# Grouping the small matrix products of a state-space scan and a chunk gate between the large ones

## The chip, the cores and the metric

The kernel runs on one core of a Trainium2 chip. The metric is the device time of one execution in microseconds, as the median of several runs; the profile is of one execution by itself, taken by the hardware profiler.

## The reference

One decoder layer is computed for 256 new prompt positions and for 8 sequences with 8 new tokens each, 320 tokens in all. Everything is float32. The two parts of the layer:

```python
h = rms_norm(x, norm_mix_pre)
a_u, a_v, z, xbc, dt_raw = split(h @ w_in)
gate_out = gelu(a_u) * (tril(W_s) @ layer_norm(gelu(a_v)) + b)      # 16 heads, chunks of 128
ssm_out  = group_norm(ssd(silu(conv(xbc)), dt) * silu(z))           # 32 heads of 64, 4 groups, state 128
x = x + rms_norm([gate_out | ssm_out] @ w_out)
x = x + rms_norm(conv_ffn(rms_norm(x)))                             # 2048 -> 2 x 5632 -> 2048
```

The state-space part (`ssd`) is the recurrence h_t = exp(dt_t a) h_{t-1} + dt_t x_t B_t^T, y_t = h_t C_t, in chunks of 128 positions. With the decays within a chunk as a matrix, y of a chunk is (C B^T * decay) (dt x) plus C times the state that the chunk begins with. The prompt has two chunks and begins with a zero state, so its second chunk alone needs a state; each of the 8 sequences brings a state of its own (8 x 32 x 64 x 128 numbers) and has one short chunk. A group of 8 heads shares its B and C.

## The kernel before, in words

Channels lie on the partitions and the 320 tokens in the free dimension. Weights pass through the kernel once, in slabs of 128 x 1024 numbers (512 KB): `slab` loads one from SP's queue into `wraw`, ScalarE rounds it to `whi` (L119), VectorE makes the rest `wlo` (L121); each of the three has three buffers. `accumulate` (L130 to L132) turns a block of 128 x 128 weights into three products with 320 columns, `whi` x hi, `whi` x lo, `wlo` x hi, which keep float32's precision on the faster format. A slab is 24 such large products. `project` runs one projection of 512 columns, `chunk_out` one part of `w_out` or `ffn_w_down`; `pd` and `ps` are their PSUM banks (`mm`, four). All other products, in plain float32 and in two passes each, go to four banks of their own (`ms`, `misc`).

What isn't a large product is written as generators: `gate_mix(g)` for four heads of the gate, `ssd(g)` for a group of eight heads of the scan, and others. They wait in a list `bg`, and `tick` runs the first of them up to its next `yield`. `project` and `chunk_out` call `tick` once or more (`rate`) behind each slab. So the number of `yield`s settles behind which slab a small product stands in TensorE's order. A scheduler then places each engine's instructions by their priority in the program and its own estimates; each engine works through its own in that order, and waits in it.

The parts that the change and the prediction's steps touch:
- `gate_mix`: for each of four heads, products of the chunk weights with v (L663, L664, bank `sg`), then VectorE's and ScalarE's work on `s` and its split in hi and lo. It yields behind every second head. The last group's call is finished without ticks in between.
- `ssd`, begin: the tokens are transposed (`xt_ps`), C B^T goes to `cb`, and the eight state tiles `st` of the group (two for each `i`, 256 KB each) are asked for on SP's queue. There are eight buffers.
- `ssd`, `with_c(i, st)` (L812): C of the sequences times the states of one pair, four products of 32 array columns each, accumulated in the bank `yo_ps` over i = 0..3. Behind the last, VectorE puts the result into `xdt` (L822).
- `decays(hl)`: the decay matrix of one head. `load_sums` brings the sums of a pair of heads (`cs`, three buffers, 320 KB, SP's queue); VectorE takes differences (L844), ScalarE the exponential (L846), VectorE multiplies by `cb` (L848). For each pair ScalarE and GpSimd make `cpx` (L837, L838, two buffers).
- `products(j)` (L859, bank `y_ps`): y of a pair of heads, each head on 64 of the array's columns, in four terms; VectorE then writes y (L869).
- `decayed(1, 1)` on GpSimd (L788), s1 times decay on GpSimd (L880), and `final` (L885, bank `fin_ps`): the last state's product and VectorE's sum with s1 (L887), and the store of s1 from ScalarE's queue (L888).
- `heads_out`: the projection for z, in whose evacuation `finish(tasks[g])` runs what is left of the group's scan.

Of the kernel before, what the change touches and what calls it, by code (L numbers as in the profile page):

```python
# [34 lines left out]
def hybrid_step(  # L35
# [21 lines left out]
    def misc(name):  # L57
        return ms.tile([P, 512], F32, tag="ms", name=name)
# [283 lines left out]
    def split(hi, lo, x, scale=None):  # L342

        if scale is None:
            act.copy(hi, x)
            dve.tensor_tensor(out=lo, in0=x, in1=hi.bitcast(F32), op=ALU.subtract)
        else:
            made = act.activation(hi, x, AF.Copy, scale=scale).ins
            dve.scalar_tensor_tensor(out=lo, in0=x, scalar=scale, in1=hi.bitcast(F32), op0=ALU.mult, op1=ALU.subtract)
            return made  # L350

    def out_parts(pool_, name):
        return (pool_.tile([P, 4, NT], F32R, tag=f"{name}hi", name=f"{name}hi"),
                pool_.tile([P, 4, NT], F32R, tag=f"{name}lo", name=f"{name}lo"))
# [7 lines left out]
    def by_head(ap):  # L362
        return ap.rearrange("p (h d) -> p h d", d=64)
# [7 lines left out]
    with ExitStack() as mctx:  # L371
# [145 lines left out]
        with tc.tile_pool(name="gp", bufs=1) as gp:  # L517
# [124 lines left out]
            def gate_mix(g, uf, res):  # L642
                wT = gp.tile([P, 4, P], F32, tag="wT", name="wT", bufs=1)
                w8 = gp.tile([NS, 4, TS], F32, tag="w8", name="w8", bufs=1)
                bs = gp.tile([P, 4, P], F32, tag="bs", name="bs", bufs=1)
                with tc.issue_after(after_v[-1]):
                    pool.dma_start(wT, gate_wT[:, 4 * g:4 * g + 4, :])
                    pool.dma_start(w8, gate_w8[:, 4 * g:4 * g + 4, :])
                    pool.dma_start(bs, gate_b_s[0:1, 4 * g:4 * g + 4, :].broadcast_to([P, 4, P]))
                yield  # L650
                with tc.issue_after(rsqrt_ins[1]):
                    dve.tensor_tensor(out=wT, in0=wT, in1=upper.unsqueeze(1).to_broadcast([P, 4, P]), op=ALU.mult)
                    for j in range(4):
                        dve.tensor_tensor(out=wS[:NS, j], in0=w8[:, j].unsqueeze(1).to_broadcast([NS, NB, TS]),
                                          in1=upper_s[:NS].rearrange("p (b t) -> p b t", b=NB), op=ALU.mult)
                yield
                hi, lo = out_parts(hp, "o")
                res += hi, lo
                for j in range(4):
                    fs = slice(512 * g + P * j, 512 * g + P * j + P)  # L660
                    ps = misc("sg")
                    for c in range(2):
                        pe.matmul(ps[:, P * c:P * c + P], vt[:, c, fs], wT[:, j, :], start=True, stop=True)  # L663
                    pe.matmul(ps[:, NP:NT], vt[:, 2, fs], wS[:, j].rearrange("p b t -> p (b t)"), start=True, stop=True)  # L664
                    s = tp.tile([P, NT], F32, tag="ev", name="s", bufs=2)
                    dve.tensor_tensor(out=s[:, :NP].rearrange("p (c t) -> p c t", c=2),
                                      in0=ps[:, :NP].rearrange("p (c t) -> p c t", c=2),
                                      in1=bs[:, j, :].unsqueeze(1).to_broadcast([P, 2, P]), op=ALU.add)
                    dve.tensor_tensor(out=s[:, NP:].rearrange("p (b t) -> p b t", b=NB),
                                      in0=ps[:, NP:NT].rearrange("p (b t) -> p b t", b=NB),  # L670
                                      in1=bs[:, j, :TS].unsqueeze(1).to_broadcast([P, NB, TS]), op=ALU.add)
                    dve.tensor_tensor(out=s, in0=s, in1=uf[:, j, :], op=ALU.mult)
                    split(hi[:, j, :], lo[:, j, :], s)
                    if j % 2:
                        yield

            spare_pads = op.tile([P, 4, NT], F32, tag="xs", name="xs_pads", bufs=2).rearrange("p k n -> p (k n)")
            spare_pads = [spare_pads[:, LP * i:LP * i + LP] for i in range(3)]
# [23 lines left out]
        with tc.tile_pool(name="sd", bufs=1) as sd:  # L702
# [24 lines left out]
            def ssd(g):  # L727
# [58 lines left out]
                def decayed(i, c):  # L786
                    xde = sd.tile([P, 512], F32, tag="xde", name="xde", bufs=1)
                    pool.tensor_tensor(out=by_head(xde), in0=by_head(xdt[:, c, :]),  # L788
                                      in1=dec[:, i, h0:h0 + 8].unsqueeze(2).to_broadcast([P, 8, 64]), op=ALU.mult)
                    return xde  # L790
# [16 lines left out]
                def with_c(i, st):  # L807

                    for r in range(2):
                        for h in range(2):  # L810
                            row = 64 * r + 32 * h
                            pe.matmul(ps_yo[row:row + 32, :256], cms[:, 4 * h + i, :], st[h][:, 256 * r:256 * r + 256],  # L812
                                      start=i == 0, stop=i == 3, tile_position=(0, row))

                for i in range(4):
                    yield
                    with_c(i, sts[i])
                    yield

                for r in range(2):  # L820
                    at = slice(64 * r, 64 * r + 64)
# [9 lines left out]
                def decays(hl):  # L831
                    j, i = hl // 2, hl % 2
                    at = places(hl)
                    if i == 0:
                        cs = load_sums(j)
                        cpx = sd.tile([P, 2, P], F32, tag="cpx", name="cpx", bufs=2)
                        act.activation(cpx, cs[:, :, at[1][0]:at[1][0] + P], AF.Exp)  # L837
                        pool.tensor_tensor(out=cpx, in0=cpx, in1=cT[:, g, P:2 * P].unsqueeze(1).to_broadcast([P, 2, P]),  # L838
                                           op=ALU.mult)
                    else:  # L840
                        cs, cpx = made[hl - 1][1:]
                    m = cs[:, i]
                    for c, (o, n) in enumerate(at):
                        dve.tensor_scalar(out=m[:, o:o + n], in0=m[:, o:o + n], scalar1=nda[:, c, h0 + hl:h0 + hl + 1],  # L844
                                          scalar2=0.0, op0=ALU.add, op1=ALU.min)
                    act.activation(m, m, AF.Exp)  # L846
                    o = NS * (hl // 4)
                    dve.tensor_tensor(out=m, in0=m, in1=cb[:, o:o + NT], op=ALU.mult)  # L848
                    made[hl] = m, cs, cpx

                def products(j):

                    ps = misc("y_ps")
                    pair = [(i, *made[2 * j + i]) for i in range(2)]

                    def both(cols, w, x, **flags):
                        for i, m, _, cpx in pair:
                            hl = 2 * j + i
                            pe.matmul(ps[64 * i:64 * i + 64, cols], w(hl), x(hl, m, cpx), tile_position=(0, 64 * i), **flags)  # L859

                    def hs(hl):
                        return slice(64 * hl, 64 * hl + 64)
                    c0, c1, sm = (slice(o, o + n) for o, n in places(2 * j))
                    both(slice(0, P), lambda hl: xdt[:, 0, hs(hl)], lambda hl, m, cpx: m[:, c0], start=True, stop=True)
                    both(slice(P, NP), lambda hl: xdt[:, 1, hs(hl)], lambda hl, m, cpx: m[:, c1], start=True, stop=False)
                    both(slice(P, NP), lambda hl: s1[:, hs(hl)], lambda hl, m, cpx: cpx[:, hl % 2, :], start=False, stop=True)
                    both(slice(NP, NT), lambda hl: xdt[:, 2, hs(hl)], lambda hl, m, cpx: m[:, sm], start=True, stop=True)
                    y = xs[:, j, :]
                    dve.scalar_tensor_tensor(out=y, in0=y, scalar=d_col[:, 4 * g + j:4 * g + j + 1], in1=ps[:, :NT],  # L869
                                             op0=ALU.mult, op1=ALU.add)  # L870
                for j in range(5):
                    for i in range(2):
                        if j < 4:
                            decays(2 * j + i)
                        if j and i == 0:
                            products(j - 1)
                        yield

                x1d = decayed(1, 1)
                pool.tensor_tensor(out=by_head(s1), in0=by_head(s1),  # L880
                                   in1=dec[:, 2, h0:h0 + 8].unsqueeze(2).to_broadcast([P, 8, 64]), op=ALU.mult)

# [7 lines left out]
                if g == 3:  # L890
                    rest.append(final())
                else:
                    yield
                    yield
                    for _ in final():
                        pass

            tasks = [ssd(g) for g in range(4)]
            res = [[] for _ in range(4)]
# [402 lines left out]
```

## Time and profile before

| | |
|---|---|
| median of 3 runs | 1789.76 us (1789.74 to 1791.35) |
| the profiled execution | 1790.97 us, span 1789.3 us |
| TensorE busy | 1775.5 us (99%) |
| VectorE busy | 1191.2 us (67%) |
| ScalarE busy | 794.3 us (44%) |
| GpSimd busy | 276.6 us (15%) |
| granted clock of TensorE | 0.998 |
| bytes moved | 303.83 MB, 170 GB/s on the mean |

The span goes from the first to the last instruction; the time of the execution is somewhat longer. In the profile PE is TensorE's matrix products, PEld its weight loads, DVE VectorE, ACT ScalarE, POOL GpSimd, SP the engine whose queue issues most loads. A float32 product has two records, one for each pass. The scan (`ssd`) runs from about 430 to 730 us, between projections and parts of `w_out`; the gate from about 265 to 435 us.

### The profile page before, as it was taken

Reading aid. Unit: us, or ns where it says so; the run is one execution under the profiler, and the core shown is the slowest. Engines: PE = TensorE matmul, PEld = TensorE weight load, DVE = VectorE, ACT = ScalarE, POOL = GpSimd, SP = SyncE. Lnnn points to the kernel's source line nnn. Section 1 sums busy time; section 2 is a strip of 40 time slices with the busy share of each in tenths; the row PEclk is TensorE's granted clock in tenths of the full one; section 3 lists DMA queues with packets and bytes.
Section 4 is the critical chain, followed back from the end, with each engine's and each line's share of the span. In section 5 each row is a group of like instructions: output and inputs, shape, how many; then the busy total and the mean of one; then the engine's idle time right before and its main releaser. Section 6 shows DMA issues by size and latency. Waiting matters only on the chain.

```text
span 1789.3 us, 31254 instructions
## 1 busy us (share of the span) xinstructions
PE 1775.5 (99%) x12241; PEld 1744.7 (98%) x12241; DVE 1191.2 (67%) x2058; ACT 794.3 (44%) x1101; POOL 276.6 (15%) x591
## 2 busy tenths in 40 slices
PE   9999999999999999999999999999999999999998
PEld 9999999999999898999999999999999999999997
DVE  7448664557867778577866675767666575656565
ACT  6343455333535364445645434443434343433334
POOL 2003200000210111002322212121101020101004
PEclk9999999999999999999999999999999999999999
DMA  7455544445664644454565656566554444444442
GB/s 246 144 165 165 189 148 153 153 153 179 226 198 147 201 154 151 142 170 153 161 196 191 206 181 202 182 197 206 183 185 154 153 147 153 156 149 149 154 156 95
DMA packets 228082, 303.83 MB, mean 170 GB/s; under 512 B 17408, under 2 KB 149856, under 8 KB 227744
## 3 DMA queue, kind: packets, MB, share of 16 engines
q1 hardware_dynamic: 216288, 281.89, 49.4%
q10 hardware_dynamic: 10160, 15.47, 2.4%
q0 software_dynamic: 1488, 4.49, 0.8%
q8 instruction: 96, 1.57, 0.4%
q14 instruction: 50, 0.41, 0.1%
HBM read 284.23 MB, written 17.58 MB: 169 GB/s over the span
## 4 chain that ended last, share of the span: by engine, by line
PE 92%; DVE 4%; DMA 1%; issue 1%; ACT 1%; POOL 0%; SPq 0%; DVEq 0%; ACTq 0%; POOLq 0%
PE ps L130 19%; PE ps L132 19%; PE ps L131 19%; PE pd L130 10%; PE pd L132 10%; PE pd L131 10%; DVE wlo L121 1%; PE y_ps L859 1%; PE yo_ps L812 1%; PE tsum L264 0%; PE sg L663 0%; PE up_ps L1152 0%; DMA wraw<-in_w_in 0%; DVE acc_mix L998 0%; PE xt_ps L360 0%
## 5 line engine op out<-in xcount | busy, mean ns | idle before, releaser
L121 DVE TENSOR_TENSOR wlo<-wraw,whi 128x1024 fp32r<-128x1024 f32 x472 | 588.7, 1248 | 385.3 <-ACT whi L119 382.6
L119 ACT CAST whi<-wraw 128x1024 fp32r<-128x1024 f32 x472 | 494.2, 1047 | 726.1 <-PE ps L131 430.7
L130 PE MATMUL ps<-h_hi,whi 128*128 128x320 f32 x2528 | 784.5, 311 | 2.8 <-DVE dtf L430 2.1
L131 PE MATMUL ps<-h_lo,whi 128*128 128x320 f32 x2528 | 780.4, 309 | 0.0
L132 PE MATMUL ps<-h_hi,wlo 128*128 128x320 f32 x2528 | 779.4, 309 | 0.5 <-DVE wlo L121 0.2
L130 PEld LDWEIGHTS ps<-h_hi,whi 128*128 128x128 f32 x2528 | 474.6, 188 | 8.4 <-issue 3.8
L131 PEld LDWEIGHTS ps<-h_lo,whi 128*128 128x128 f32 x2528 | 474.8, 188 | 1.5 <-issue 0.5
L132 PEld LDWEIGHTS ps<-h_hi,wlo 128*128 128x128 f32 x2528 | 474.1, 188 | 2.0 <-DVE wlo L121 1.8
L130 PE MATMUL pd<-fhi,whi 128*128 128x320 f32 x704 | 217.3, 309 | 0.0
L132 PE MATMUL pd<-fhi,wlo 128*128 128x320 f32 x704 | 217.3, 309 | 0.0
L131 PE MATMUL pd<-flo,whi 128*128 128x320 f32 x704 | 217.3, 309 | 0.0
L130 PE MATMUL pd<-ohi,whi 128*128 128x320 f32 x448 | 140.8, 314 | 0.0
L131 PE MATMUL pd<-olo,whi 128*128 128x320 f32 x448 | 139.2, 311 | 0.0
L132 PE MATMUL pd<-ohi,wlo 128*128 128x320 f32 x448 | 138.9, 310 | 0.0
L131 PEld LDWEIGHTS pd<-flo,whi 128*128 128x128 f32 x704 | 132.2, 188 | 0.7
L132 PEld LDWEIGHTS pd<-fhi,wlo 128*128 128x128 f32 x704 | 132.2, 188 | 0.0
L130 PEld LDWEIGHTS pd<-fhi,whi 128*128 128x128 f32 x704 | 132.2, 188 | 0.0
L216 DVE TENSOR_TENSOR acc_ffn<-acc_ffn,pd 128x320 f32<-128x320 f32 x160 | 77.5, 484 | 35.8 <-PE pd L132 34.8
L130 PEld LDWEIGHTS pd<-ohi,whi 128*128 128x128 f32 x448 | 84.1, 188 | 4.0 <-issue 2.5
L132 PEld LDWEIGHTS pd<-ohi,wlo 128*128 128x128 f32 x448 | 84.1, 188 | 0.6 <-issue 0.6
L131 PEld LDWEIGHTS pd<-olo,whi 128*128 128x128 f32 x448 | 84.2, 188 | 0.2 <-issue 0.2
L1049 POOL COPY ptf<-pad 128x2 f32<-128x2 f32 x88 | 20.8, 238 | 406.5 <-DVE pad L1037 406.0
(297 smaller groups left out, 1588.1 us busy)
## 6 DMA issues: line engine op xcount, KB each, us to landing
wraw<-in_ffn_w_up SPq DMA_DIRECT2D x176, 512.0 KB, 3.5
wraw<-in_w_in SPq DMA_DIRECT2D x144, 512.0 KB, 3.5
wraw<-in_ffn_w_down SPq DMA_DIRECT2D x88, 512.0 KB, 3.3
wraw<-in_w_out SPq DMA_DIRECT2D x64, 512.0 KB, 3.3
st<-in_state_ssm SPq DMA_DIRECT2D x64, 256.0 KB, 3.8
out_ssm_state_sample<-st ACTq DMA_DIRECT2D x32, 256.0 KB, 2.7
cs<-dacs_d SPq DMA_DIRECT2D x16, 320.0 KB, 3.5
xr<-in_xT SPq DMA_DIRECT2D x4, 640.0 KB, 4.6
```

The costliest lines, as they stand in the source:

```text
L119: act.copy(hi[:, :m], raw[:, :m])
L121: dve.tensor_tensor(out=lo[:, :m], in0=raw[:, :m], in1=hi[:, :m].bitcast(F32), op=ALU.subtract)
L130: pe.matmul(ps, whi, xhi, start=first, stop=False)
L131: pe.matmul(ps, whi, xlo, start=False, stop=False)
L132: return pe.matmul(ps, wlo, xhi, start=False, stop=last).ins
L216: dve.tensor_tensor(out=acc[:, nb, :], in0=acc[:, nb, :], in1=ps[:, :NT], op=ALU.add)
L812: pe.matmul(ps_yo[row:row + 32, :256], cms[:, 4 * h + i, :], st[h][:, 256 * r:256 * r + 256], start=i == 0, stop=i == 3, tile_position=(0, ...
L859: pe.matmul(ps[64 * i:64 * i + 64, cols], w(hl), x(hl, m, cpx), tile_position=(0, 64 * i), **flags)
L1049: pool.tensor_copy(ptf[:, k, :], pad[:, 256:258])
```

## The change

It touches only where the generators yield and in which order they do their steps:
- `gate_mix` does four heads behind one tick instead of two and two.
- `ssd` lets five ticks pass, and then does `with_c` for all four pairs of states at once, and yields once. Before, there was a `yield` ahead of and behind each.
- y is made for two pairs (four heads) at once: the decays of four heads, one head per tick, one more tick, then `products` of both pairs. Before, the products of a pair stood behind the first decay of the next pair.
- `decayed(1, 1)` stands ahead of the decays instead of behind the last products.
- The two `yield`s ahead of `final` are gone, one stands behind it; so in the first three groups the last state's product stands right behind the second two pairs' y.

```diff
@@ gate_mix
                     split(hi[:, j, :], lo[:, j, :], s)
-                    if j % 2:
-                        yield
+                yield
@@ ssd
+                yield from repeat(None, 5)
                 for i in range(4):
-                    yield
                     with_c(i, sts[i])
-                    yield
+                yield
...
-                for j in range(5):
-                    for i in range(2):
-                        if j < 4:
-                            decays(2 * j + i)
-                        if j and i == 0:
-                            products(j - 1)
+                x1d = decayed(1, 1)
+                for j in range(0, 4, 2):
+                    for hl in range(2 * j, 2 * j + 4):
+                        decays(hl)
                         yield
-
-                x1d = decayed(1, 1)
+                    yield
+                    products(j)
+                    products(j + 1)
...
                 if g == 3:
                     rest.append(final())
                 else:
-                    yield
-                    yield
                     for _ in final():
                         pass
+                    yield
```

## The prediction

> **What bounds the kernel now.** I read the page first: the shares of busy time, and the chain that ended last.
>
> ```profile
> span 1789.3 us, 31254 instructions
> PE 1775.5 (99%) x12241; PEld 1744.7 (98%) x12241; DVE 1191.2 (67%) x2058; ACT 794.3 (44%) x1101; POOL 276.6 (15%) x591
> PE 92%; DVE 4%; DMA 1%; issue 1%; ACT 1%; POOL 0%; SPq 0%; DVEq 0%; ACTq 0%; POOLq 0%
> ```
>
> TensorE is the chain: 92% of it, and 99% busy. So the time is the length of TensorE's stream of products, and an edit is worth what it takes from that stream or adds to it. The second view, the waits of PE, bears this out: the wait for VectorE's weight halves (`wlo`, which feed every large product) comes once in the whole span.
>
> ```profile
> PE ps L132 <- DVE wlo L121: 0.2, 1, 0.2
> ```
>
> "Busy" doesn't tell what a product costs, since its record overlaps with its neighbours'. The distance from start to start does, so the third view is PE's timeline around a lone burst of each kind: y of one pair of heads (L859), then C times one pair of states (L812). Columns: start, length, engine, line, operation, tiles, shapes.
>
> ```profile
> 483.25 0.31 PE L132 MATMUL pd<-ohi,wlo 128*128 128x320 f32 x1
> 483.49 0.66 PE L859 MATMUL y_ps<-cs,xdt 128*64 128x128 f32 x8
> 483.98 0.39 PE L859 MATMUL y_ps<-cpx,s 128*64 128x128 f32 x4
> 484.20 0.28 PE L859 MATMUL y_ps<-cs,xdt 128*64 128x64 f32 x4
> 484.41 0.41 PE L130 MATMUL pd<-ohi,whi 128*128 128x320 f32 x1
> 484.66 0.31 PE L131 MATMUL pd<-olo,whi 128*128 128x320 f32 x1
> ```
>
> ```profile
> 478.53 0.31 PE L132 MATMUL pd<-ohi,wlo 128*128 128x320 f32 x1
> ...
> 478.97 0.31 PE L132 MATMUL pd<-ohi,wlo 128*128 128x320 f32 x1
> 479.21 0.64 PE L812 MATMUL yo_ps<-st,cb_cms 128*32 128x256 f32 x8
> 479.78 0.41 PE L130 MATMUL pd<-ohi,whi 128*128 128x320 f32 x1
> 480.03 0.31 PE L131 MATMUL pd<-olo,whi 128*128 128x320 f32 x1
> ```
>
> Large products start 0.147 us apart (three steps from 478.53 to 478.97, the two rows between left out). From the last one to a burst on part of the array's columns (`128*64`, `128*32`) it is 0.24 us, 0.09 more; from the first large one behind the burst to the second it is 0.25, 0.10 more. Those are edges, paid once per burst however much lies inside.
>
> **The change part by part.** The price of a lone burst is the distance from the product before it to the second one behind it, less the two steps of 0.147 that would be there anyway.
> - y of a pair: 484.66 - 483.25 = 1.41, less 0.29: 1.12 us. Its content: the two passes over `cpx` take 484.20 - 483.98 = 0.22 us, so the three terms with 128 columns take 0.66, and the fourth, with 64, takes 0.11: 0.77 us. A pair that joins another's burst costs its content alone and saves 0.35 us.
> - C times a pair of states: 480.03 - 478.97 = 1.06, less 0.29: 0.77 us. Content: two passes with 256 columns, twice the 0.22 of 128 columns, so 0.44 us, an estimate, since nowhere in this trace do two pairs of states follow each other. Saving 0.33 us. Bounds: 0.19 if only the two measured edges go, 0.34 at most.
>
> In the order of the built kernels the bursts do come together. The C products stood in 16 bursts (4 groups of 4) and get 4: 12 x 0.33 = 3.9 us less. y had 16 pairs in 18 bursts, since two pairs of the second group are torn: a first product of theirs stands ahead of the rest.
>
> ```profile
> 580.92 0.31 PE L131 MATMUL pd<-olo,whi 128*128 128x320 f32 x1
> 581.16 0.43 PE L859 MATMUL y_ps<-cs,xdt 128*64 128x128 f32 x2
> 581.52 0.42 PE L132 MATMUL pd<-ohi,wlo 128*128 128x320 f32 x1
> 581.78 0.32 PE L130 MATMUL pd<-ohi,whi 128*128 128x320 f32 x1
> ...
> 583.85 0.31 PE L132 MATMUL pd<-ohi,wlo 128*128 128x320 f32 x1
> 584.09 0.54 PE L859 MATMUL y_ps<-cs,xdt 128*64 128x128 f32 x5
> ...
> 585.00 0.41 PE L130 MATMUL pd<-ohi,whi 128*128 128x320 f32 x1
> 585.25 0.31 PE L131 MATMUL pd<-olo,whi 128*128 128x320 f32 x1
> ```
>
> This pair costs 581.78 - 580.92 - 0.29 = 0.57 and 585.25 - 583.85 - 0.29 = 1.11, together 1.68 us, 0.56 more than an untorn one; I take the second (at 587.79) as the same. Before: 16 x 1.12 + 2 x 0.56 = 19.0 us. After, 8 bursts of two pairs: 8 x (1.12 + 0.77) = 15.1 us. That is 3.9 us less.
>
> The gate's blocks need no such model. In three groups they come two by two; in the last group all four stand together already:
>
> ```profile
> 326.75 0.31 PE L132 MATMUL ps<-h_hi,wlo 128*128 128x320 f32 x1
> 326.89 0.61 PE L663 MATMUL sg<-wT,vt 128*128 128x128 f32 x4
> ...
> 328.38 0.31 PE L131 MATMUL ps<-h_lo,whi 128*128 128x320 f32 x1
> ...
> 429.35 0.31 PE L132 MATMUL pd<-ohi,wlo 128*128 128x320 f32 x1
> ...
> 432.32 0.31 PE L131 MATMUL ps<-h_lo,whi 128*128 128x320 f32 x1
> ```
>
> Two blocks: 328.38 - 326.75 - 0.29 = 1.34 us; four: 432.32 - 429.35 - 0.29 = 2.68, just twice that. These products use the whole array (`128*128`), and there is no edge to save (326.75 to 326.89 is a usual step). Three mergers: 0, and at most 0.03 us. The state's last product (L885), moved behind the second y burst, is of the same kind: 0. VectorE gets four blocks' work in one place instead of two; the wait row for `wlo` (0.2 us) says that it has room, and in the last group it does it so already.
>
> Here a page speaks against the change. C times a pair loads its weights at these times:
>
> ```profile
> 479.21 0.16 PEld L812 LDWEIGHTS yo_ps<-st,cb_cms 128*32 128x32 f32 x8 [0.19 <-issue]
> ```
>
> All eight weight loads, those of the second pass too, end at 479.37, while the first pass's products still run. The Trainium skill ("TensorE: Matmul & The Clock Gate", Part 3, "The mechanism") says that weight loads overlap with running products only where the row group differs; here all rows are used and only the column groups differ. By that rule a second pair would start when the first is through, and the sum below would be 4.5 us instead of 7.4; the row, with loads under products of the same rows, is against it. What such a mechanism would cost here stands as the first rival.
>
> What the grouping can add are waits. The row for `wlo` gives the cover of all that happens on other engines. In the built order VectorE makes a slab's `wlo` mostly two slabs ahead, 48 large products or 7.1 us.
> - **States.** One C burst needs all eight state tiles and hands them back at once, so that the next group's loads stand together on SP's queue (before: spread over four bursts), with three slabs of weights among and behind them. The rows: busy time by stretch (PE, PEld, DVE, ACT, POOL, clock, DMA share, GB/s), the page's groups, its DMA issues.
>
> ```profile
> 470.00:505.00 35.00, 35.00 (x282) 32.15 (x281) 31.27 (x68) 18.08 (x32) 7.69 (x13) 1.00 0.64 203
> ...
> L121 DVE TENSOR_TENSOR wlo<-wraw,whi 128x1024 fp32r<-128x1024 f32 x472 | 588.7, 1248 | 385.3 <-ACT whi L119 382.6
> L119 ACT CAST whi<-wraw 128x1024 fp32r<-128x1024 f32 x472 | 494.2, 1047 | 726.1 <-PE ps L131 430.7
> ...
> st<-in_state_ssm SPq DMA_DIRECT2D x64, 256.0 KB, 3.8
> ```
>
> The loads go out behind the C burst of the group before, over 200 large products (30 us) ahead of their use, and land in 3.8: no wait for them. For the weights behind them: the pile is 8 x 256 KB and one slab of 512 KB, 2.6 MB. At the stage's 203 GB/s, where the DMA engines were 64% busy, that takes 13 us; the slab behind it is needed 144 products, 21 us, after the burst, and its conversion takes 1.05 + 1.25 us. 6 us are left: 0.
> - **The second y burst.** `cs` has three buffers for four pairs, so the fourth pair's load waits on SP for the first y burst. Before, that was the first pair's own burst, three slabs ahead of the fourth pair's. Now, in the first group, two slabs (48 products, 7.1 us) lie between the two bursts; in the others it is three or twelve.
>
> ```profile
> L844 DVE TENSOR_SCALAR cs<-cs,nda x96: 243/276/865, 451.8 to 715.3; 128x128 f32<-128x128 f32 x64, 128x64 f32<-128x64 f32 x32
> L846 ACT ACTIVATE cs<-cs x32: 454/470/474, 455.8 to 715.8; 128x320 f32<-128x320 f32 x32
> L848 DVE TENSOR_TENSOR cs<-cs,cb_cms x32: 472/485/1028, 457.2 to 716.3; 128x320 f32<-128x320 f32 x32
> DMA to landing us min/median/max: 3.3/3.5/8.1
> ...
> 484.52 0.38 SPq L744 DMA_DIRECT2D cs<-dacs_d  x1
> ...
> L216 DVE TENSOR_TENSOR acc_ffn<-acc_ffn,pd 128x320 f32<-128x320 f32 x160 | 77.5, 484 | 35.8 <-PE pd L132 34.8
> ```
>
> The load goes out 484.52 - 483.49 = 1.0 us after the burst's start and lands 3.5 later. Then VectorE has 6 x 0.28 for two heads, ScalarE 0.47, VectorE 2 x 0.49, and on VectorE one `wlo` (1.25) and three accumulations (0.48 each) stand between: 5.8 us, and 1.0 + 3.5 + 5.8 = 10.3 with all in a row. The first accumulation is done while the load is under way, and ScalarE works beside VectorE: 9.4. The fourth pair's products come 1.9 (first burst) + 7.1 + 0.8 (third pair) = 9.8 us after the first burst's start. So a wait of 0 to 0.5 us, with the longest landing (8.1) up to 5.1. I take 0.4, by the median of the landings.
>
> - **The state's sum.** L887 (s1 plus the last product) now stands on VectorE right behind the second burst's y, and waits for GpSimd's s1 times decay (L880), which waits for that burst. Queued behind it on VectorE are the next group's differences, the evacuation of its transposes, for whose banks PE waits, and a `wlo`; on ScalarE's queue the store of s1 waits for the sum, with exponentials and a `whi` behind it. In the sum 0: a slab of 24 products, 3.5 us, lies between the burst and the transposes, against GpSimd's 1.0. What it costs without that cover is the third rival.
>
> Sum: 3.9 + 3.9 - 0.4 = 7.4 us less. The profiled execution took 1790.97 us (its span of 1789.3 and 1.7 around it), 1.2 above the median of the runs, 1789.76. So 1783.6 of the one, and 1782.4 of the other.
>
> **The rivals.**
> 1. *Every pair pays for its weights again.* Only the edges go, 0.19 us per burst: C 12 x 0.19 = 2.3; y after is 8 x (1.12 + 0.93) = 16.4, so 2.6 less; with the wait of 0.4, 4.5 us: 1785.3. For it: no trace of two pairs of states in a row. Against: the weight row above, and y, in whose bursts each new term follows in the usual 0.11 per pass.
> 2. *The fourth pair's chain is late.* The load of `cs` takes the longest of its landings, 8.1 us, and the first group waits 5.1: 7.8 - 5.1 = 2.7 us less, 1787.1. For it: VectorE is 31.27 of 35 us busy in that stage. Against: the median of 3.5.
> 3. *VectorE is held behind the state's sum, and the next slabs come late: slower.* GpSimd's wait and product take
>
> ```profile
> L880 POOL TENSOR_TENSOR s<-s,dec x4: 1043/1044/2061, 498.4 to 722.2; 128x512 f32<-128x512 f32 x4
> ```
>
> 1.0 to 2.1 us behind the burst, in three groups (the fourth's sum comes at the very end). Behind it VectorE has up to the next `wlo` 11 x 0.28, 2 x 0.48, the sum and two evacuations of half a `wlo`'s elements (3 x 0.62, an estimate from its 1.25) and the `wlo`: 7.2 us. That `wlo` is needed 72 products, 10.6 us, behind the burst, which leaves 10.6 - 7.2 - 2.1 = 1.3 us (the transposes on PE add to it). What VectorE is late beyond that goes straight to PE. It ends slower when that is over (7.4 + 3.6) / 3 = 3.7 us in each group; at 4, it is 12 - 7.4 = 4.6 us more: 1794.4. For it: VectorE's 31.27 of 35 us. Against: the row of waits, 0.2 us in all, with the same work in the same stage.
> 4. *The bursts don't come together.* The built order shows that they do; this has no chance of its own.
>
> **How the numbers follow.** The forecast 0.75, rival 1 0.10, rival 2 0.10, rival 3 0.05. About 0.2%, 3.6 us, is what a measurement of this kernel can tell from no change. Faster by more: the forecast, rival 1 and a part (0.02) of rival 2, where the landing is only somewhat late: 0.87. Within it: the rest of rival 2: 0.08. Slower: 0.05. The likeliest is 1782.4. The forecast's own ends: below, C at its upper bound (0.1 more), no wait (0.4) and half of what the runs of before lie apart (1791.35 - 1789.74, so 0.8): 1781.1; above, C halfway to its lower bound (12 x 0.07 = 0.8), a wait of 0.5 and the same 0.8: 1784.1. The range goes on over rival 1 to 1786.0, and leaves out the most of rivals 2 and 3.
>
> **What would show it.** In the new profile's timeline of PE: a C burst of 32 records and a y burst of 32 with one pair of edges; second to fourth pair at 0.44 us each, not 0.58; gate bursts of four at 2.68. PE's wait for `cs` (L847) at the first group's second y burst: under 1 us. PE's row for `wlo` still under 1 us. If PE's own stream is 7 us shorter and the span isn't, a wait has come in its place, and rivals 2 and 3 say where. Wrong at the root it would be if lone edges cost less inside bursts than the distances make them.

## The result: the small products got shorter by what their edges cost

| comparison | before, median | after, median | after / before, 95% interval |
|---|---|---|---|
| the two kernels alone | 1789.74 us (5 runs) | 1782.30 us (5) | 0.9955 (0.9944 to 0.9965) |
| beside the parts of the change | 1791.48 us (27) | 1782.98 us (5) | 0.9950 (0.9938 to 0.9963) |
| beside the spread-out first group | 1791.22 us (9) | 1782.22 us (5) | 0.9950 (0.9937 to 0.9962) |

The change is faster by 7.4 us between the medians of the first row (6.3 to 10.0 by its interval). 1782.4 was predicted. The two later comparisons give 8.5 and 9.0 us. The profiled execution of the changed kernel took 1781.46 us, its span 1779.8. First its page, as of the kernel before:

```profile
span 1779.8 us, 31264 instructions
PE 1767.1 (99%) x12241; PEld 1746.0 (98%) x12241; DVE 1189.6 (67%) x2058; ACT 794.8 (45%) x1101; POOL 275.5 (15%) x591
```

The same 12241 products, PE still 99% busy, and the span shorter: the stream itself got shorter. Next PE's timeline around a C burst, and the weight loads of that burst (start, length, engine, line, operation, tiles, shapes):

```profile
471.40 0.31 PE L132 MATMUL pd<-ohi,wlo 128*128 128x320 f32 x1
471.64 1.93 PE L811 MATMUL yo_ps<-st,cb_cms 128*32 128x256 f32 x32
473.51 0.41 PE L130 MATMUL pd<-ohi,whi 128*128 128x320 f32 x1
473.76 0.31 PE L131 MATMUL pd<-olo,whi 128*128 128x320 f32 x1
...
471.64 1.45 PEld L811 LDWEIGHTS yo_ps<-st,cb_cms 128*32 128x32 f32 x32 [0.19 <-issue]
473.51 0.19 PEld L130 LDWEIGHTS pd<-ohi,whi 128*128 128x128 f32 x1 [0.41 <-issue]
```

All 32 records stand together, with one pair of edges: 0.24 us ahead and 0.25 behind, as at a lone pair before. The price, reckoned as in the prediction, is 473.76 - 471.40 - 0.29 = 2.07 us (2.06 with unrounded starts, which is used from here on). A lone pair cost 0.77, so each further pair costs (2.07 - 0.77) / 3 = 0.43. The weight loads run on through the burst and end at 473.09, 0.42 us ahead of the next large product: nothing waits for them.

The y burst of two pairs, and the second of the first group, behind which the last state's product now stands:

```profile
484.02 0.31 PE L132 MATMUL pd<-ohi,wlo 128*128 128x320 f32 x1
484.27 0.66 PE L858 MATMUL y_ps<-cs,xdt 128*64 128x128 f32 x8
...
486.22 0.32 PE L131 MATMUL pd<-olo,whi 128*128 128x320 f32 x1
...
492.98 0.31 PE L132 MATMUL pd<-ohi,wlo 128*128 128x320 f32 x1
493.22 0.66 PE L858 MATMUL y_ps<-cs,xdt 128*64 128x128 f32 x8
...
494.91 1.12 PE L883 MATMUL fin_ps<-xde,btok 128*128 128x512 f32 x2
...
496.02 0.31 PE L131 MATMUL pd<-olo,whi 128*128 128x320 f32 x1
```

One costs 486.22 - 484.02 - 0.29 = 1.91 us where 1.89 was forecast; the other, with the last state's product, 2.75, which is 1.89 and the 0.86 that a product of the same shape costs by itself (the state's first, `s_ps`, at 447.61 us in the kernel before). A gate burst of four heads begins behind the large product at 320.18:

```profile
320.18 0.31 PE L132 MATMUL ps<-h_hi,wlo 128*128 128x320 f32 x1
320.33 0.61 PE L663 MATMUL sg<-wT,vt 128*128 128x128 f32 x4
...
323.15 0.31 PE L131 MATMUL ps<-h_lo,whi 128*128 128x320 f32 x1
```

323.15 - 320.18 - 0.29 = 2.68 us, twice a burst of two heads. Last the waits of PE, columns: engine, product and line, what it waited for, us in total, times, longest:

```profile
...
PE ps L130 <- DVE dtf L430: 1.3, 1, 1.3
...
PE ps L130 <- ACT whi L119: 0.7, 1, 0.7
PE cb_ps L771 <- DVE xdt L751: 0.6, 1, 0.6
...
```

Of the seven rows none is a wait for `wlo` and none for `cs`. New is the row for `cb_ps`: the next group's C B^T (`cb_ps`, at 501.9 us) waits for VectorE to empty a bank of transposes.

### The profile page after: what moved, and what is told of

Same layout as the page of the kernel before. It is cut to its first block, busy times and chain, and to the rows that moved or that the text cites. A ratio compares the mean times of both kernels' runs of the same rounds, so it can differ in the third digit from the quotient of the medians.

```text
span 1779.8 us, 31264 instructions
## 1 busy us (share of the span) xinstructions
PE 1767.1 (99%) x12241; PEld 1746.0 (98%) x12241; DVE 1189.6 (67%) x2058; ACT 794.8 (45%) x1101; POOL 275.5 (15%) x591
## 4 chain that ended last, share of the span: by engine, by line
PE 94%; DVE 3%; DMA 1%; issue 1%; ACT 1%; POOL 0%; SPq 0%; DVEq 0%; ACTq 0%; POOLq 0%
PE ps L130 20%; PE ps L132 20%; PE ps L131 19%; PE pd L130 10%; PE pd L131 10%; PE pd L132 10%; DVE wlo L121 1%; PE y_ps L858 1%; PE tsum L264 0%; PE sg L663 0%; PE yo_ps L811 0%; PE up_ps L1149 0%; DMA wraw<-in_w_in 0%; PE xt_ps L360 0%; DVE cv L399 0%
```

## The experiments

**The parts alone.** Three kernels are the one before with one part of the change each, run beside the changed kernel on one chip. The times that the expectations give count from 1789.7 us; the kernel before took 1791.48 in this comparison and 1790.81 and 1791.22 in the later ones, so it is the differences from it that are compared.

C alone:

```diff
+                yield from repeat(None, 7)
                 for i in range(4):
-                    yield
                     with_c(i, sts[i])
-                    yield
+                yield
```

> The kernel before with one part of the change alone: C times the states of all four pairs in one burst per group (16 bursts become 4); y and the gate stay as they were. Theory (a lone burst pays 0.33 us that a joined pair doesn't): 12 x 0.33 = 3.9 us less than before, 1785.8 by the median of 1789.7. Rival (every pair pays for its weights again, only the two measured edges go): 12 x 0.19 = 2.3 less, 1787.4. Rival (the gain of the whole change lies in y and in the order of the other engines): 0, 1789.7.

Measured: 1788.32 us, ratio to before 0.9981 (0.9973 to 0.9990), so 1.8 to 4.8 us less. The time holds both 3.9 and the rival's 2.3; the trace doesn't. PE's timeline of this kernel:

```profile
476.29 0.31 PE L132 MATMUL pd<-ohi,wlo 128*128 128x320 f32 x1
476.53 1.93 PE L812 MATMUL yo_ps<-st,cb_cms 128*32 128x256 f32 x32
478.40 0.41 PE L130 MATMUL pd<-ohi,whi 128*128 128x320 f32 x1
478.65 0.31 PE L131 MATMUL pd<-olo,whi 128*128 128x320 f32 x1
```

2.07 us again, where weights paid per pair would have made it 0.77 + 3 x 0.58 = 2.5. Four such bursts are 8.25 us from start to start, against 16 x 0.77 = 12.3. Part of that doesn't arrive in this execution's time: PE waits 1.5 us at the norm's sums (at 645 us), where it waited 0.3 in the profile of the kernel before.

y alone (the diff of the change in its y part, with the state's decay and the last product moved; `with_c` and the gate as before):

> The kernel before with the second part alone: y of two pairs together, the states' decay ahead of it, the last state's product behind it; C and the gate stay as they were. In the built order two of the second group's pairs are torn again by the ticks that C keeps, so 16 pairs stand in some ten bursts, not eight. Theory (0.35 us per joined pair, and the torn ones lose some of it): about 3.3 us less, 1786.4. Rival (edges of 0.19 alone): 8 x 0.19 - 0.6 = 0.9 to 1.5 less, 1788.5. Rival (a wait of VectorE behind the state's sum eats it): 1789.7 or more.

Measured: 1788.33 us, 0.9982 (0.9973 to 0.9991), 1.6 to 4.8 us less; 3.2 between the medians. From start to start in its trace, y takes 16.8 us without its waits, against 19.0, and two of C's pairs happen to stand together (0.3 less). Three waits of about 0.5 us stand against that: in the first group's second y burst, at the next group's C B^T, and one where a pair is torn:

```profile
584.29 0.43 PE L859 MATMUL y_ps<-cs,xdt 128*64 128x128 f32 x2 [0.49 <-DVE cs L848]
584.66 0.41 PE L132 MATMUL pd<-ohi,wlo 128*128 128x320 f32 x1
585.00 0.54 PE L859 MATMUL y_ps<-cs,xdt 128*64 128x128 f32 x5
```

So of y's own 3.9 us not much over half arrives in this kernel's stream; the rest needs C's ticks gone, with which the tearing goes. The time agrees with 3.3, but its interval is too wide to settle what makes it up.

The gate alone:

```diff
-                    if j % 2:
-                        yield
+                yield
```

> The kernel before with the third part alone: four heads of the gate behind one tick instead of two and two. Theory (products on the whole array have no edge): 0, at most 0.03 us, 1789.7. Rival (any burst between the large products has an edge of its own, of some 0.33 us): three mergers, 1.0 us less, 1788.7. Rival (VectorE's four blocks in one place make the next weight halves late): longer than before, with a wait of PE for the weight halves in the stage from 300 to 430 us.

Measured: 1790.37 us, 0.9994 (0.9985 to 1.0003): no difference that shows, but the rival's 1.0 us less lies in the interval too; the time can't tell them apart. The trace does. Summed from start to start, the gate's products take 10.73 us in seven bursts before and 10.72 in four here. A burst on the whole array has no edge of 0.33 us. The second rival isn't seen either: PE has no wait for the weight halves between 300 and 430 us (its one, 0.5 us, is at 859).

The changed kernel beside them:

> The changed kernel itself, beside its three parts on one chip. If the parts add up (3.9 + 3.3 + 0, and the torn pairs' 0.6 come back when C's ticks are gone): 7.4 to 7.8 us less than before, 1782.3. If parts depend on each other in another way, the difference from their sum says how much.

Measured: 1782.98 us, 8.5 less between the medians; the parts give 3.16 + 3.15 + 1.11 = 7.4, the gate's 1.11 of them within the noise. They add up within what these runs can tell.

**What an edge is.** The changed kernel with extra products, whose results nothing uses, ahead of and inside its bursts. `large` is one product on the whole array.

```diff
+                def large(out, n):
+                    pe.matmul(out, hT[0][:, 0, :P], hT[0][:, 0, :n], start=True, stop=True)
...
+                gap = misc("gap")
                 for i in range(4):
                     with_c(i, sts[i])
+                    if i < 3:
+                        large(gap[:, :256], 256)
...
+                    if j % 2 == 1:
+                        large(ps[:, NT:], 192)
```

> The changed kernel with 20 added products on the whole array, of the large products' kind, inside the bursts: one of 256 columns behind the first, second and third pair of each C burst (12), one of 192 columns between the two pairs of each y burst (8). Their results are used nowhere. By columns against the large products' 320 columns in 0.147 us they take 12 x 0.12 + 8 x 0.09 = 2.1 us themselves. Theory (a burst on part of the columns pays 0.33 to 0.35 us each time that products on the whole array stand on both sides): 12 x 0.33 + 8 x 0.35 = 6.8 more, so 8.9 over the changed kernel, 1791.2. Rival (only the two measured edges of 0.19): 3.8 more, 5.9 over it, 1788.2. Rival (the gain came from the other engines' order, which stays): 2.1 over it, 1784.4.

The control has the three products of a C burst, and the one of a y burst, ahead of it:

> The control: the changed kernel with the same 20 added products, ahead of the bursts instead of inside. Theory: their own 2.1 us and no edge, 1784.4. Rival (each added product costs a place of its own, wherever it stands): as much as with the products inside, 1791.2.

Measured: 1793.88 us inside, ratio to before 1.0014 (1.0005 to 1.0023), and 1786.22 ahead, 0.9972 (0.9960 to 0.9983). 7.7 us lie between the medians, where 6.8 was forecast: products that cost little ahead of the bursts take away the whole gain of the change when they stand inside them. From the kernel before, the one is 3.1 us over (1.5 forecast), the control 4.6 under (5.3). From start to start, waits not counted, the bursts of the two kernels differ by 4.05 us in C and 2.78 in y, 6.8 in all, as forecast; the rest of the 7.7 lies outside these products' own prices. The control's trace has the products themselves as forecast (three in 0.35 us: 472.49 - 472.05 = 0.44, less the 0.09 that the burst's edge has anyway).

```profile
472.05 0.51 PE L807 MATMUL gap<-h_hi 128*128 128x256 f32 x3
472.49 1.93 PE L814 MATMUL yo_ps<-st,cb_cms 128*32 128x256 f32 x32
```

Is the edge one of the tile's width or of the number format? Three more kernels have products of other kinds at the places inside the C bursts (none in the y bursts): the large products' format on 64 columns and on 32 of the array, and plain float32 on the whole array.

```diff
+                def narrow(out, n):
+                    pe.matmul(out[:64], hT[0][:, 0, :64], hT[0][:, 0, :n], start=True, stop=True, tile_position=(0, 0))
...
+                    if i < 3:
+                        narrow(gap[:, :256], 256)
```

> The changed kernel with 12 added products inside the C bursts, at the same places and of the same format and columns (256) as those on the whole array, but on 64 of the array's columns. Their own time is 12 x 0.12 = 1.4 us at most. Theory A (the edge stands between the whole array and a part of it): no edge, 1.4 over the changed kernel, 1783.7. Theory B (any change of the tile's width has the edge, 32 to 64 columns too) and theory C (the change of format has it): 12 x 0.33 more, 5.4 over it, 1787.7. B and C are told apart by the gate's bursts, which change the format on the whole array.

> The changed kernel with 12 added products inside the C bursts as before, in the large products' format with 256 columns, but on 32 of the array's columns, the width of the C products. Read from the burst's length (2.06 us without them, 3.26 with the ones on 64 columns, 3.43 with the ones on the whole array). Theory B (a change of the tile's width has the edge): 2.06 and at most 3 x 0.12, 2.1 to 2.4 us. Theory C (the change of format has it): about 3.3 us, as with 64 columns.

> The changed kernel with 12 added products inside the C bursts, in plain float32 like the C products themselves (two passes of 256 columns), on the whole array. By the last state's product (512 columns in 0.86 us) one takes 0.43 us itself. Theory B (a change of the tile's width has the edge of 0.34): 2.06 + 3 x (0.43 + 0.34) = 4.4 us a burst. Theory C (the change of format has it, and there is none here): 2.06 + 3 x 0.43 = 3.35 us.

The timelines of PE, one fence for each kernel, in this order: whole array inside, 64 columns, 32 columns, whole array in float32:

```profile
472.29 0.64 PE L814 MATMUL yo_ps<-st,cb_cms 128*32 128x256 f32 x8
472.86 0.38 PE L807 MATMUL gap<-h_hi 128*128 128x256 f32 x1
473.18 0.64 PE L814 MATMUL yo_ps<-st,cb_cms 128*32 128x256 f32 x8
```

```profile
472.13 0.64 PE L814 MATMUL yo_ps<-st,cb_cms 128*32 128x256 f32 x8
472.70 0.33 PE L807 MATMUL gap<-h_hi 128*64 128x256 f32 x1
472.96 0.64 PE L814 MATMUL yo_ps<-st,cb_cms 128*32 128x256 f32 x8
```

```profile
475.28 0.64 PE L814 MATMUL yo_ps<-st,cb_cms 128*32 128x256 f32 x8
475.85 0.30 PE L807 MATMUL gap<-h_hi 128*32 128x256 f32 x1
476.08 0.64 PE L814 MATMUL yo_ps<-st,cb_cms 128*32 128x256 f32 x8
```

```profile
474.64 0.64 PE L814 MATMUL yo_ps<-st,cb_cms 128*32 128x256 f32 x8
475.20 0.70 PE L807 MATMUL gap<-cT,btok 128*128 128x256 f32 x2
475.83 0.64 PE L814 MATMUL yo_ps<-st,cb_cms 128*32 128x256 f32 x8
```

| between two pairs | from pair to pair | above 0.43 | its own time | left: the edge |
|---|---|---|---|---|
| whole array, the large products' format | 0.89 | 0.46 | 0.12 | 0.34 |
| 64 columns, that format | 0.83 | 0.40 | 0.12 | 0.28 |
| 32 columns, that format | 0.80 | 0.37 | 0.12 | 0.25 |
| whole array, float32 | 1.19 | 0.76 | 0.43 | 0.33 |

A product's own time is an estimate by its columns: 256 of 320 in 0.147 us, and half of the 0.86 of 512 columns in float32.

Theory A falls as it stood: 64 columns inside 32 cost 0.28 us beyond their own time, where it gave none. The kernel took 1787.70 us (0.9982, 0.9973 to 0.9991), 3.1 us under the kernel before; A gave 6.0 under it, B and C 2.0. Theory C can't carry it alone: in the last row the format doesn't change, and 0.33 stays (4.36 us a burst, where B gave 4.4 and C 3.35; one run, 1793.88 us). But for the burst with 32 columns B gave 2.1 to 2.4 us, and it takes 2.06 + 3 x 0.37 = 3.17 (one run, 1789.84 us), near C's 3.3: at the same width a lone product of the other format costs 0.25 us beyond its own time. So the change between 32 columns and the whole array has an edge by itself, without a change of format. For 64 columns inside 32 that isn't shown, since 0.25 of the 0.28 us come without any change of width. Whether those 0.25 us come from the format, or from one product alone in one of four column groups that otherwise work side by side, is left open; on the whole array the gate shows that the format has none.

One sign goes with the edges in these traces: the weight load isn't ahead of its product. Here is that of the lone product on 32 columns:

```profile
475.85 0.11 PEld L807 LDWEIGHTS gap<-h_hi 128*32 128x32 f32 x1 [0.41 <-issue]
```

It starts with its product (475.85), and so do the loads at the edges of a C burst (471.64 and 473.51 above). Between large products the load starts a step ahead (319.74 for the product at 319.88 in the changed kernel), and so it does where a gate burst begins (320.18 for 320.33; behind the burst it is 0.03 us). Whether the late load is what makes the edge no run here tests.

**The waits of the first group.** Between its first and second y burst lie 48 large products, 24 more up to the next group's transposes. All profiled runs of this order have waits here, and they differ from run to run. The first theory was that VectorE is late because its sum of the state waits for GpSimd. This is VectorE and GpSimd in the changed kernel:

```profile
494.68 1.82 POOL L837 TENSOR_TENSOR cpx<-cpx,cT 128x256 f32<-128x256 f32 x1 [4.39 <-ACT cpx L836]
496.47 1.04 POOL L878 TENSOR_TENSOR s<-s,dec 128x512 f32<-128x512 f32 x1
497.54 0.69 DVE L885 TENSOR_TENSOR s<-s,fin_ps 128x512 f32<-128x512 f32 x1 [0.71 <-POOL s L878]
501.90 0.71 PE L771 MATMUL cb_ps<-cT,bT 128*128 128x128 f32 x4 [0.60 <-DVE xdt L751]
```

To take that wait away, the decay goes to a buffer of its own, which doesn't wait for y:

```diff
                 x1d = decayed(1, 1)
+                s1d = sd.tile([P, 512], F32, tag="x4", name="s1d", bufs=1)
+                pool.tensor_tensor(out=by_head(s1d), in0=by_head(s1), in1=..., op=ALU.mult)
...
-                pool.tensor_tensor(out=by_head(s1), in0=by_head(s1), in1=..., op=ALU.mult)
...
-                    dve.tensor_tensor(out=s1, in0=s1, in1=ps, op=ALU.add)
+                    dve.tensor_tensor(out=s1, in0=s1d, in1=ps, op=ALU.add)
```

> The changed kernel with GpSimd's s1 times decay written to a buffer of its own ahead of the decays, so that it no longer waits for y; TensorE's order is the same. It takes away VectorE's wait for GpSimd behind the second y burst (0.71 us in the first group), and if that is what made VectorE late, PE's wait of 0.60 us for the evacuation of the next group's transposes too: 0.6 us less than the changed kernel, 1781.7. Rival (VectorE is late there by its own load of differences): the wait of PE stays, 1782.3. The time alone can't tell 0.6 us apart, the rows of waits can.

Measured: 1782.53 us, 0.9951 (0.9938 to 0.9963), as the changed kernel. What the theory gave didn't come: VectorE's sum no longer waits (third row), but PE's wait is still there, and another one came.

```profile
490.35 0.29 DVE L843 TENSOR_SCALAR cs<-cs,nda 128x128 f32<-128x128 f32 x1 [0.99 <-DMA cs<-dacs_d]
494.88 0.90 PE L858 MATMUL y_ps<-cs,xdt 128*64 128x128 f32 x7 [0.69 <-PE y_ps L858]
498.58 0.67 DVE L886 TENSOR_TENSOR s<-s1d,fin_ps 128x512 f32<-128x512 f32 x1
PE cb_ps L771 <- DVE xdt L751: 0.8, 1, 0.8
```

The first row is the fourth pair's sums, landed late, and the second the wait for them inside the second y burst. In the changed kernel beside the spread-out group (below) VectorE's sum doesn't wait for GpSimd either, and PE waits 1.2 us for VectorE:

```profile
498.80 0.67 DVE L885 TENSOR_TENSOR s<-s,fin_ps 128x512 f32<-128x512 f32 x1
```

So GpSimd isn't needed for this wait. In both these executions the load of the sums is late, though, which holds VectorE too; in the first profile it isn't, and there the 0.71 us for GpSimd can be the cause. No run settles that. In four profiled runs with this order (us behind the first burst's start; the wait is the burst's price above 2.75):

| run | VectorE begins on the fourth pair | wait inside the second y burst |
|---|---|---|
| the first profile after | 4.98, not held by the load (ScalarE, which waits for the same load, begins at 4.78) | 0 |
| beside the spread-out group | 5.33 | 0.48 |
| beside the parts | 5.55 | 0.70 |
| decay apart | 6.10 | 1.25 |

From about 4.85 us on, what the load is later goes to PE one to one. The three kernels with products added in the C bursts alone lie on the same line (5.36, 5.41 and 5.68 us behind; waits of 0.53, 0.59 and 0.83).

The later landing isn't chance alone. The pages' issue rows give the median landing of these loads, first before, then after, and SP's queue shows two of them issued together behind the first y burst, where the kernel before issued one (484.52 us):

```profile
cs<-dacs_d SPq DMA_DIRECT2D x16, 320.0 KB, 3.5
cs<-dacs_d SPq DMA_DIRECT2D x16, 320.0 KB, 4.3
485.30 1.14 SPq L743 DMA_DIRECT2D cs<-dacs_d  x2
```

The other profiles of this order have 4.1 to 4.9; of the parts, C alone has 4.3, y alone 4.2, the gate alone 3.8. Which of the loads that now stand together does it, no run separates. The remedy would be distance:

```diff
-                yield from repeat(None, 5)
+                yield from repeat(None, 5 if g else 1)
...
-                    yield
+                    yield from repeat(None, 1 if g else (1,3)[j // 2])
                     products(j)
...
-                    yield
+                    yield from repeat(None, 1 if g else 3)
```

> The changed kernel with the first group spread out: its C burst stands one tick behind the state's first product instead of five, its two y bursts lie 72 large products apart instead of 48, and the next group's transposes 48 behind the second y burst instead of 24. In six profiled runs with the changed kernel's order the first group's second y burst waited 0 to 1.3 us for the chain behind the load of the fourth pair's sums, and C B^T of the next group 0.4 to 1.6 us for VectorE's evacuation behind it. Theory (both follow from the distance): both waits go, 1 to 2 us less than the changed kernel beside it, about 1781.3. Rival (VectorE is full in that stage and is late wherever the burst stands): the waits move to another place and the time stays, 1782.5.

> The changed kernel beside the one with the first group spread out, on one chip: 1782.5, and in its profile a wait of 0 to 1.3 us at the first group's second y burst and of 0.4 to 1.6 us at C B^T behind it.

Measured: 1781.72 us, 0.9947 (0.9934 to 0.9961), beside 1782.22 of the changed kernel: 0.5 less, which these runs can't tell from none. First a row of the changed kernel, then the waits of the spread-out one:

```profile
PE cb_ps L771 <- DVE xdt L751: 1.2, 1, 1.2
```

```profile
PE tsum L264 <- DVE ssq L282: 0.9, 1, 0.9
PE cb_ps L771 <- DVE xdt L751: 0.6, 1, 0.6
```

And the spread-out kernel's busy time in the stretch of that wait (columns as in the prediction):

```profile
500.00:510.00 10.00, 9.42 (x64) 8.52 (x62) 9.29 (x19) 1.60 (x2) 5.19 (x2) 1.00 0.50 159
```

The wait for the fourth pair is gone (its burst is at 2.75 again, against 3.22 beside it); that for the transposes is halved, not gone, with twice the distance; and a wait at the norm's sums (`tsum`) is 0.5 us longer, start to start. The first half of the theory holds, of the second the rival: VectorE is full there (9.29 of 10 us busy), and part of what is saved comes back at the next place. Between the two profiles 0.55 us is gained from the first changed product to behind the norm's sums; another 1.1 us lies ahead of every product whose place differs (PE's wait for `dtf`, 1.2 us in the one and none in the other).

## Why the prediction was right, point by point

- **C, 3.9 us:** 4 x 2.06 = 8.2 us against 12.3, 4.05 less from start to start. The estimate that the prediction rested on, a second pair at 0.44, measured 0.43; the lower bound, edges of 0.19 alone, is out. Its source was right as well: the two passes over 128 columns, doubled.
- **y, 3.9 us:** 19.05 to 15.12, 3.93 less, waits not counted (the first profile has none in y). The torn pairs of the second group became whole, as the built order said.
- **The gate and the last product, 0:** 10.73 to 10.72 us, and 2.75 for a y burst with it.
- **States, 0:** right. PE waits neither for `st` nor for `wlo` in the first profile, though the loads behind the first C burst take up to 6.0 us to land, where the prediction had 3.8.
- **The fourth pair's wait, 0.4 us (0 to 0.5, 5.1 at most):** the mechanism and its chain were right, the landing was undersized, since it was taken from the kernel before: a median of 3.5 us there, 4.3 after the change. Nor did the 0.4 follow from the working: its better chain, 9.4 us against 9.8 us of cover, leaves no wait. The prediction had the load land 4.5 us behind the burst and 4.9 us of work behind that; by the table, work and distance leave it 4.85 us, and it landed between at most 4.78 and 6.10. So the wait is 0 in the first profile and 0.5 to 1.25 in the others. Its bounds for the likeliest case were too narrow, its outer one was not reached.
- **The state's sum, 0:** the cover that it named, the 24 products up to the transposes, isn't enough by 0.6 us in the first profile, by 0.2 and 1.2 in the changed kernel's other two. The prediction counted GpSimd's product and not the next group's `cpx` that stands ahead of it (1.82 us in the row above). But the wait is there where the sum doesn't wait for GpSimd, too (1.2 us above), so VectorE's own queue, with the late load ahead of it, is enough to make it late; what it was in the first profile stays open. This is the third rival's place, at a price of 0.2 to 1.2 us and once instead of three times, far from its 4 us per group.
- **What the sum did not have:** transposes, C B^T and the state's product come in fewer pieces too, about 0.9 us less from start to start without the wait. That offsets the wait in the first profile. So that the first comparison came within 0.1 us of the forecast is in part luck: a gain that the sum left out and waits that it put too low stand against each other, and the later comparisons gave 8.5 and 9.0. In the scan's stretch the two profiled executions differ by 7.95 us (295.61 and 287.66); their spans differ by 9.5, of which 1.7 lie ahead of every changed instruction (PE goes on behind its wait for `dtf` at 194.93 and 193.24 us; 0.8 of the 1.7 is that wait, 2.1 and 1.3 us).
- **Rival 1:** the Trainium skill ("TensorE: Matmul & The Clock Gate", Part 3, "The mechanism") says in one sentence that weight loads overlap with running products "only when row_grp differs"; in another it also lets them go ahead into a background weight buffer. By the first a further pair would cost 0.58 us. The 32 loads above belong to products on all rows, overlap with them throughout, and the pair costs 0.43: the trace doesn't agree with the first, and whether the second is what happens no run here shows.
- **The edge itself:** the Trainium skill ("TensorEngine Tiling (Array Packing)", "Key Properties") says that a change of the tiling mode drains TensorE, without a price. That such a change costs time the trace bears out between 32 columns and the whole array, with 0.33 to 0.34 us. Between 32 and 64 columns it doesn't settle it: of those 0.28 us 0.25 come at one and the same width, and these are not in that rule.

## What to carry to other kernels

Where TensorE is the chain, compare the start-to-start price of a lone burst with its content: what is left is an edge, and bursts of the same tile width should be joined until it is paid once. Products on the whole array may be left scattered (the gate: 10.73 and 10.72 us). Joining also moves the loads that refill what a burst frees: count from the burst to the next use with a later landing than the median of the kernel before (here 3.5 us became 4.3), and look at what else is queued on the engine that has to work on it.

## What the runs showed of the hardware

Not expected: a product on 64 columns inside a burst on 32 costs 0.28 us beyond its own 0.12 (an estimate by its columns), and one on the same 32 columns in another format 0.25. So what a lone product pays isn't only an edge between the whole array and a part of it. Nor expected was that loads of one kind, issued at the same place, land over a microsecond apart from one execution to the next (at most 4.78 to 6.10 us behind the burst), although the changed kernel's medians differ by less than one.
